# Streaming encoder layer, one core: the last query blocks' weight loads are asked for together, and the first head's second loads are placed behind them

## The chip, the cores and the metric

The kernel runs on one core of one Trainium2 chip. The metric is the device time of one execution in microseconds. Before the change the median of three runs is 2940.57 us (2935.65 to 2942.43).

## The reference, cut to what matters

One layer of a chunk-causal encoder, for 2048 new frames of one stream (16 tiles of 128 rows) and 16 frames of each of 8 running streams (one more tile, the sample tile). All arithmetic is float32.

```
h = rmsnorm(x, g_mix_pre)
proj = h @ w_in                       # 1024 -> q 512 | k 512 | v 512 | u_val 512 | u_gate 512
att = band_attention(q, k, v)         # 8 heads of 64, band of 9 chunks of 64, learned bias
u = u_val * sigmoid(u_gate)
c = depthwise_conv(u, width=31) + conv_b
c = silu(layernorm(c, cln_g, cln_b))
x = x + rmsnorm(concat(att, c) @ w_out, g_mix_post)
...                                   # cross-attention over 256 memory tokens, then a SwiGLU FFN
```

The outputs hold the new x, the keys and values of the band, and the convolution's last rows.

## The kernel before, in words

**Products.** A float32 product is made of three fast ones. Each operand is split into a high part (a rounding copy) and a low part (the rest), and high·high, high·low and low·high are added in PSUM. `mm3` issues the three, on lines 284, 285 and 286 of the profile. A block of weights, 128 columns by 1024 rows, goes through `wload`: a load on SP's queue into a buffer `wf` (L274), a rounding copy on ScalarE (ACT) into `wh` (L278), and the rest on POOL into `wl` (L279). There are three `wf` buffers and four each of `wh` and `wl`, used in turn. So a load waits until the block three earlier has been split, and a split waits until the products of the block four earlier are done.

**The projection** (`phase_proj`) takes the token tiles in three groups. The last group holds tiles 12 to 15 and the sample tile, in two parts of three and two tiles. For each group come the convolution's inputs (blocks 12 to 19 of `w_in`), the values, and then keys and queries. In the last group these are eight blocks, four of keys (called K0 to K3 here) and four of queries (Q0 to Q3), each of two heads. For each block and part `qk` multiplies (24 products of 384 columns, then 24 of 256), evicts the result from PSUM with ACT (L713 for keys, L707 for queries) and VectorE (L714, L708), and stores it in DRAM (L733); keys are also turned for the output (L721 to L726).

**The convolution** of the last group runs beside this, one step at a time: VectorE's taps are L524, POOL's and ACT's L534 and L533. Its end, `conv_norm`, is handed out in stages behind the products of Q1 and Q2. For each of the five tiles it transposes (L539, TensorE), takes statistics (L541 and L543 on VectorE, L299 and L302 on POOL), normalizes (L547), transposes back (L551), scales and applies tanh (L554, L557 on ACT) and multiplies (L558 on VectorE). POOL then stores the tile (L559). The last three of its five results lie at kilobytes 6 to 12 of the buffer `sbF`, which the second and third `wf` buffers also use.

**Attention's beginning.** For each head, `head_load` brings q, k, the low part of k and v back from DRAM (L809, L810). For the first head this is done in two parts: tiles 0 to 11 at the start of the last group, tiles 12 to 15 right after Q0. Scores are L894, the softmax is L822 on VectorE and L824 on ACT, its transposes are L911, their evictions L912 and L913, the products with the values L924. A sample stream's softmax uses the same lines with 272 columns, and bias rows that eight small loads (L937) bring. Those rows lie over the end of the second z tile of the convolution and the first columns of its tanh tile, so they can come only when the last L558 has run.

**What sets the order.** The program is written with a framework that places every instruction on its engine's queue, by the order of the code, by priorities and by its own model of time. Each engine then runs its queue strictly in that order. A load on SP that waits holds up all loads behind it. `issue_after(x)` asks that what is written inside it stand behind x.

Of the kernel before, what the change touches and what calls it, by code (L numbers as in the profile page):

```python
# [20 lines left out]
NPT = 16  # L21
# [116 lines left out]
class Build:  # L138
# [309 lines left out]
    def phase_proj(self):  # L448
        nc, A = self.nc, self.A
# [49 lines left out]
        def pump(q, n):  # L499
            while n > 0 and q:  # L500
                try:
                    with self.tc.high_priority(offset=-LOWP):
                        next(q[0])
                    n -= 1
                except StopIteration:
                    q.pop(0)
# [69 lines left out]
        def stage():  # L576
            if stages:
                with self.tc.issue_after(self.last_product.ins):
                    for i, n in stages.pop(0):
                        for _ in range(n):  # L580
                            next(staged[i], None)

        def stages_of(tiles, cts, tag, x):
            staged[:] = [conv_norm(t, cts, i * P, tag, x) for i, t in enumerate(tiles)]
            n = len(tiles)
            first = [tuple((i, 1) for i in range(x, min(n, x + 2))) for x in range(0, n, 2)] + [()]
            rest = [()] + [tuple((i, 2) for i in range(x, min(n, x + 2))) for x in range(0, n, 2)]
            stages.extend(r + f for r, f in zip(rest, first))
# [5 lines left out]
        for gi, subs in enumerate(GROUPS):  # L594
# [4 lines left out]
            t0 = tiles[0]  # L599
            hs = nxt  # L600
            if last:
                first = self.head_tiles(0)
# [131 lines left out]
                                                   sp[:, :, :npc].bitcast(F32))  # L734

            if last:
                for which, j in [(1, j) for j in range(4)] + [(0, j) for j in range(4)]:
                    blk = self.wload(A["w_in"][which * 4 + j])
                    for x in range(2):
                        qk(which, j, blk, x)  # L740
                        if (which, j, x) == (0, 1, 0):
                            while vq or pq:
                                pump(vq or pq, 1)
                            stages_of(tiles, cts, "nt", "x")
                        stage()
                    if (which, j) == (0, 0):
                        self.head_load(0, first, t0, NPT)
                        self.head0 = first
                break

            for j in range(3):
                for which in (1, 0):
                    blk = self.wload(A["w_in"][which * 4 + j])
# [1029 lines left out]
```

## Time and profile before

| | |
|---|---|
| three runs, median | 2940.57 us (2935.65, 2940.57, 2942.43) |
| the profiled execution | 2934.83 us |
| its span | 2933.1 us |
| TensorE's mean granted clock in it | 0.994 |
| the last group's end and attention's first head | about 560 to 670 us of the span |

In the rows of a timeline stand the start, the duration, the engine, the line and the operation, what is written and read, the shapes and how many follow each other; in brackets the idle time of that engine just before, and what ended it. PE is TensorE, DVE is VectorE, ACT is ScalarE, POOL is GpSimd, and SPq is SP's queue of DMA issues. In a row of stretches (start and end) stand the length, the busy time and the number of instructions of each engine, TensorE's granted clock, the share of the DMA engines and GB/s. In a row of waits stand who waited, for whom, how long in all, how often, and the longest.

### The profile page before, as it was taken

What the parts mean: (1) busy time and instruction counts of PE and PEld (TensorE: products, weight loads), DVE (VectorE), ACT (ScalarE), POOL (GpSimd) and SP (SyncE); (2) the same over time, 40 slices, a digit from 0 to 9 for tenths busy, and PEclk for the clock granted to TensorE, in tenths of its full rate; (3) what the DMA queues carried; (4) which work ended last, traced back from release to release, by engine and by line L of the source; (5) the groups of instructions that cost most, each with busy time, mean ns of one, the idle gap of its engine ahead of it and who ended that gap; (6) DMA issues with size and microseconds to landing.
All of it is one profiled execution on the core that took longest, in us unless ns stands there. A gap on an engine that the chain in (4) does not pass through costs nothing. (4 is left out here: it accounts for less than half of the span.)

```text
span 2933.1 us, 45413 instructions
## 1 busy us (share of the span) xinstructions
PE 2868.2 (98%) x16740; PEld 2623.9 (89%) x16740; DVE 2058.8 (70%) x3063; ACT 1311.1 (45%) x2661; POOL 1321.0 (45%) x1213
## 2 busy tenths in 40 slices
PE   8999999979999999999999999999999999999998
PEld 8999999979988777888889999999999999888787
DVE  6697796959985335345559877787778998556665
ACT  4535455749974234232334333433344444433433
POOL 0268595820023222233336665466556776324413
PEclk9999999989999999999999999999999999999999
DMA  8735255558855665133354433544444446756764
GB/s 305 252 112 173 97 167 180 158 158 199 212 161 183 208 244 173 51 130 106 138 167 154 177 129 110 198 159 148 143 153 149 142 141 222 232 174 219 247 200 150
DMA packets 198154, 500.04 MB, mean 170 GB/s; under 512 B 18981, under 2 KB 87085, under 8 KB 189603
## 3 DMA queue, kind: packets, MB, share of 16 engines
q1 hardware_dynamic: 187211, 459.78, 48.4%
q0 software_dynamic: 10720, 37.36, 3.3%
q8 instruction: 131, 2.15, 0.3%
q14 instruction: 92, 0.75, 0.1%
HBM read 365.97 MB, written 141.81 MB: 173 GB/s over the span
## 5 line engine op out<-in xcount | busy, mean ns | idle before, releaser
L284 PE MATMUL psb<-sbr 128*128 128x384 f32 (+3 forms) x2808 | 942.1, 337 | 14.2 <-ACT sbr L278 11.0
L285 PE MATMUL psb<-sbr 128*128 128x384 f32 (+3 forms) x2356 | 806.5, 342 | 2.4 <-DVE sbr L321 2.4
L286 PE MATMUL psb<-sbr 128*128 128x512 f32 (+3 forms) x1848 | 631.1, 344 | 2.6 <-DVE sbr L1685 2.5
L284 PEld LDWEIGHTS psb<-sbr 128*128 128x128 f32 x2808 | 530.9, 189 | 44.2 <-ACT sbr L278 11.4
L286 PE MATMUL psb<-sbr,sbx 128*128 128x384 f32 (+2 forms) x1484 | 477.2, 323 | 1.1 <-POOL sbx L279 1.0
L285 PEld LDWEIGHTS psb<-sbr 128*128 128x128 f32 x2356 | 445.6, 189 | 28.6 <-DVE sbr L321 2.7
L286 PEld LDWEIGHTS psb<-sbr 128*128 128x128 f32 x1848 | 347.6, 188 | 31.4 <-DVE sbr L1685 4.6
L1485 ACT CAST sbr<-sbf 128x512 fp32r<-128x512 f32 x258 | 159.3, 621 | 283.6 <-PE psb L285 249.1
L286 PEld LDWEIGHTS psb<-sbr,sbx 128*128 128x128 f32 x1484 | 281.5, 190 | 1.8 <-POOL sbx L279 1.7
L524 DVE SCALAR_TENSOR_TENSOR psb<-sbf,psb 128x768 f32<-128x768 f32 (+1 forms) x290 | 264.6, 912 | 6.6
L1486 DVE TENSOR_TENSOR sbr<-sbf,sbr 128x512 fp32r<-128x512 f32 x258 | 241.8, 940 | 28.0 <-ACT sbr L1485 26.3
L292 PE MATMUL psb<-sbr 128*128 128x512 f32 x1004 | 246.2, 394 | 2.8 <-ACT sbr L1053 1.6
L1685 DVE TENSOR_TENSOR sbr<-sbf,sbr 128x384 fp32r<-128x384 f32 (+1 forms) x231 | 161.1, 720 | 95.3 <-ACT sbr L1684 93.9
L292 PEld LDWEIGHTS psb<-sbr 128*128 128x128 f32 x1004 | 185.2, 188 | 44.5 <-issue 2.5
L279 POOL TENSOR_TENSOR sbx<-sbf,sbr 128x1024 fp32r<-128x1024 f32 x60 | 153.0, 2552 | 72.6 <-ACT sbr L278 72.2
L1684 ACT CAST sbr<-sbf 128x384 fp32r<-128x384 f32 (+1 forms) x231 | 111.0, 497 | 166.8 <-PE psb L285 141.8
L1617 POOL TENSOR_TENSOR sbf<-sbf 128x512 f32<-128x512 f32 x77 | 107.7, 1403 | 167.2 <-DMA sbf<-in_w_down_dram 165.0
L534 POOL TENSOR_TENSOR flexb<-flexb,flexb 128x128 f32<-128x128 f32 (+1 forms) x180 | 167.8, 933 | 18.6 <-ACT flexb L533 9.3
L284 PE MATMUL psb<-sbr,sbx 128*128 128x384 f32 (+1 forms) x524 | 171.1, 329 | 0.6 <-ACT sbr L1447 0.5
L1485 ACT CAST sbx<-sbf 128x512 fp32r<-128x512 f32 x153 | 94.8, 621 | 164.3 <-PE psb L285 152.7
L292 PE MATMUL psb<-sbr,sbx 128*128 128x512 f32 x654 | 161.5, 398 | 5.3 <-DVE sbr L1251 2.2
L292 PEld LDWEIGHTS psb<-sbr,sbx 128*128 128x128 f32 x654 | 123.3, 191 | 34.9 <-DVE sbr L1251 2.9
(333 smaller groups left out, 5907.7 us busy)
## 6 DMA issues: line engine op xcount, KB each, us to landing
af<-flexb SPq DMA_DIRECT2D x33, 1344.0 KB, 5.2
sbf<-in_w_down_dram SPq DMA_DIRECT2D x154, 256.0 KB, 3.6
sbf<-af SPq DMA_DIRECT2D x90, 384.0 KB, 4.2
sbf<-in_w_gate_dram SPq DMA_DIRECT2D x66, 512.0 KB, 4.8
sbf<-in_w_up_dram SPq DMA_DIRECT2D x66, 512.0 KB, 3.3
sbf<-in_w_in_dram SPq DMA_DIRECT2D x48, 512.0 KB, 3.9
sbf<-x SPq DMA_DIRECT2D x47, 512.0 KB, 3.9
sbr<-ks SPq DMA_DIRECT2D x28, 512.0 KB, 8.8
```

The lines of the kernel that those rows point to most:

```text
L279: self.lo_engine.tensor_tensor(lo[:, :], wf[:, :], hi[:, :].bitcast(F32), ALU.subtract)
L284: nc.tensor.matmul(ps, lh, rh, start=start, stop=False, **kw)
L285: nc.tensor.matmul(ps, lh, rl, start=False, stop=False, **kw)
L286: self.last_product = nc.tensor.matmul(ps, ll, rh, start=False, stop=stop, **kw)
L292: self.last_half = nc.tensor.matmul(y[o], l, r[:, o * 512:(o + 1) * 512], start=start and x == 0, stop=stop and x == 2)
L524: nc.vector.scalar_tensor_tensor(acc if w < CW - 1 else o, src(w), cwt[:, j, w:w + 1], acc, ALU.mult, ALU.add)
L534: nc.gpsimd.tensor_tensor(o, o, v, ALU.add)
L1485: nc.scalar.copy(hs[j][:, :], src[j])
L1486: nc.vector.tensor_tensor(ls[j][:, :], src[j], hs[j][:, :].bitcast(F32), ALU.subtract)
L1617: nc.gpsimd.tensor_tensor(acc[:, :], acc[:, :], q[:, :], ALU.add if s > 0 else ALU.subtract)
L1684: nc.scalar.copy(ch[:, m], a[:, x, m])
L1685: nc.vector.tensor_tensor(cl[:, m], a[:, x, m], ch[:, m].bitcast(F32), ALU.subtract)
```

## The change

When Q0 has been projected, the weights of Q1, Q2 and Q3 are asked for together, and the loop takes them from `ready` instead of loading each at its turn. The second part of the first head's loads is written inside `issue_after` of the last of these three loads.

```diff
             if last:
+                ready = {}
                 for which, j in [(1, j) for j in range(4)] + [(0, j) for j in range(4)]:
-                    blk = self.wload(A["w_in"][which * 4 + j])
+                    blk = ready.pop(j, None) or self.wload(A["w_in"][which * 4 + j])
                     for x in range(2):
                         qk(which, j, blk, x)
...
                     if (which, j) == (0, 0):
-                        self.head_load(0, first, t0, NPT)
+                        ready = {i: self.wload(A["w_in"][i]) for i in (1, 2, 3)}
+                        with self.tc.issue_after(self.last_load.ins):
+                            self.head_load(0, first, t0, NPT)
                         self.head0 = first
```

Three lines are added, so all lines below shift by three: L809 is L812 in the changed kernel, L822 is L825, L894 is L897, L913 is L916, L937 is L940.

On SP's queue the order of the loads was, around K0's store and, further on, around the bias loads:

```order
L274 DMA sbf<-in_w_in_dram 128x1024 x2
L733 DMA ks_14_86<-sbf 128x2x384
L695 DMA out_dram<-flexb_153 8x16x512
L733 DMA ks_14_86<-sbf 128x2x128
L809 DMA sbr<-ks_14_86 64x512 x4
L733 DMA ks_15_87<-sbf 128x2x384
```

```order
L834 DMA flexb_157<-in_cache_att_v_dram 128x2x512
L937 DMA flexb_153<-toep_595 16x272 x6
L274 DMA sbf<-in_w_in_dram 128x1024
L937 DMA flexb_153<-toep_595 16x272 x2
L1038 DMA flexb_153<-cs_36_108 128x512
```

The single L274 of the second piece is Q3's load; the two of the first are Q1's and Q2's. In the changed kernel the same two places read:

```order
L274 DMA sbf<-in_w_in_dram 128x1024 x2
L733 DMA ks_14_86<-sbf 128x2x384
L695 DMA out_dram<-flexb_153 8x16x512
L733 DMA ks_14_86<-sbf 128x2x128
L274 DMA sbf<-in_w_in_dram 128x1024
L812 DMA sbr<-ks_14_86 64x512 x3
L733 DMA ks_15_87<-sbf 128x2x384
L812 DMA sbr<-ks_14_86 64x512
L813 DMA sbr<-vs_18_90 128x512
```

```order
L841 DMA sbf<-in_cache_att_kt_dram 128x4x256
L836 DMA sbf<-vsampd_149 16x512
L837 DMA flexb_157<-in_cache_att_v_dram 128x2x512
L940 DMA flexb_153<-toep_595 16x272 x8
L1041 DMA flexb_153<-cs_36_108 128x512
```

Q3's load has gone from among the bias loads to a place ahead of the first head's second loads, and those, the value rows among them, now stand behind it.

On TensorE, this is the end of Q2 before and what followed it, and then the rows just ahead of the first product of Q3 (128x384):

```order
L286 MATMUL psb<-sbr,sbx 128x256
L894 MATMUL psb<-sbr 128x256 x2
L894 MATMUL psb<-sbr 128x512 x2
L551 MATMUL psb<-ident_73,flexb_153 128x128 x4
L539 MATMUL psb<-ident_73,flexb_157 128x128 x4
L894 MATMUL psb<-sbr 128x256 x2
```

```order
L894 MATMUL psb<-sbr 128x256 x2
L551 MATMUL psb<-ident_73,flexb_153 128x128 x4
L539 MATMUL psb<-ident_73,flexb_157 128x128 x4
L551 MATMUL psb<-ident_73,flexb_153 128x128 x4
L911 MATMUL psb<-ident_73,flexb_153 128x128 x2
L551 MATMUL psb<-ident_73,flexb_153 128x128 x4
L284 MATMUL psb<-sbr 128x384
```

In the changed kernel Q3's 48 products follow Q2's directly. Inside Q3's second part stand 16 transposes of the convolution, and after it the scores begin with tile 0:

```order
L284 MATMUL psb<-sbr 128x256
L551 MATMUL psb<-ident_73,flexb_153 128x128 x4
L539 MATMUL psb<-ident_73,flexb_157 128x128
L551 MATMUL psb<-ident_73,flexb_153 128x128 x4
L539 MATMUL psb<-ident_73,flexb_157 128x128 x7
L285 MATMUL psb<-sbr 128x256
```

```order
L286 MATMUL psb<-sbr,sbx 128x256
L897 MATMUL psb<-sbr 128x128 x2
L897 MATMUL psb<-sbr 128x256 x4
L551 MATMUL psb<-ident_73,flexb_153 128x128 x4
L539 MATMUL psb<-ident_73,flexb_157 128x128 x4
L897 MATMUL psb<-sbr 128x384 x2
```

So the scores and three of the five L551 groups, which stood ahead of Q3, now stand behind it.

On VectorE of the changed kernel, the last result of the convolution (L558) and the softmax of sample stream 0 (the 272 columns that use the bias rows) stand like this among the softmax tiles (L825, 640 columns) and the evictions (L916):

```order
L825 ISA flexb_153,flexb_157<-psb,flexb_153 128x640
L825 ISA flexb_157 128x1
L558 SCALAR_TENSOR_TENSOR sbf<-flexb_153,sbf 128x512
L916 TENSOR_TENSOR sbx<-psb,sbx 128x128
L916 TENSOR_TENSOR sbr<-psb,sbr 128x512
L916 TENSOR_TENSOR sbx<-psb,sbx 128x512
L825 ISA flexb_157<-psb,flexb_153 128x640
L825 ISA flexb_157 128x1
L916 TENSOR_TENSOR sbr<-psb,sbr 128x512
L825 ISA flexb_153,flexb_157<-psb,flexb_153 128x272
```

Before, all five L558 stood ahead of Q3's evictions, and the 272-wide softmax came after the sixth softmax tile; now nine tiles stand ahead of the last L558, and ten ahead of that softmax.

## Prediction

> **What bounds the kernel now.** First the page: TensorE is busy 98% of the span, so only a stage in which it stands idle can give much.
>
> ```profile
> span 2933.1 us, 45413 instructions
> PE 2868.2 (98%) x16740; PEld 2623.9 (89%) x16740; DVE 2058.8 (70%) x3063; ACT 1311.1 (45%) x2661; POOL 1321.0 (45%) x1213
> ```
>
> All times below are us from the span's start, of this one profiled execution: 2934.83 us on the device, 2933.1 of them span. The three timed runs have a median of 2940.57 (2935.65 to 2942.43); the profiled execution lies 5.7 below it.
>
> The change touches the end of the last group's projection, so I next read the busy time by stretches of 10 us there.
>
> ```profile
> core 0: us, PE busy (x) PEld busy (x) DVE busy (x) ACT busy (x) POOL busy (x), PEclk, DMA share, GB/s
> ...
> 610.00:620.00 10.00, 9.27 (x69) 8.66 (x68) 5.42 (x15) 3.05 (x10) 1.75 (x5) 1.00 0.48 158
> 620.00:630.00 10.00, 4.21 (x24) 2.87 (x22) 7.37 (x14) 9.61 (x26) 4.84 (x12) 0.81 0.59 202
> 630.00:640.00 10.00, 0.53 (x2) 0.54 (x3) 0.69 (x1) 1.82 (x3) 1.36 (x3) 0.50 0.62 212
> 640.00:650.00 10.00, 9.00 (x43) 8.71 (x42) 0.97 (x2) 0.49 (x1) 1.85 (x1) 0.67 0.17 43
> 650.00:660.00 10.00, 9.39 (x67) 7.80 (x65) 8.43 (x28) 7.48 (x21) 1.23 (x2) 1.00 1.02 236
> 660.00:670.00 10.00, 10.00 (x93) 9.19 (x92) 9.45 (x24) 9.66 (x26) 0.00 (x0) 1.00 0.45 92
> ```
>
> TensorE does nearly nothing from 620 to 640, its granted clock falls to 0.50 and is still 0.67 on average in the stretch after. The timeline of TensorE shows what stands around that hole.
>
> ```profile
> 608.51 0.34 PE L284 MATMUL psb<-sbr 128*128 128x384 f32 x1
> ...
> 616.08 0.40 PE L894 MATMUL psb<-sbr 128*128 128x256 f32 x2
> ...
> 627.38 1.06 PE L551 MATMUL psb<-ident,flexb 128*128 128x128 f32 x4
> 639.47 0.69 PE L284 MATMUL psb<-sbr 128*128 128x384 f32 x1 [11.03 <-ACT sbr L278]
> ...
> 650.52 0.28 PE L286 MATMUL psb<-sbr,sbx 128*128 128x256 f32 x1
> ```
>
> Block Q2 (third query block) starts at 608.51. At 616.08 TensorE, done with it, starts on scores of attention's first head (L894) mixed with the convolution's transposes (L551), waits 11.03 us for the weights of Q3, and does Q3 from 639.47 to about 650.64. Whose fault that is, the other engines' timelines and SP's waits say:
>
> ```profile
> 638.37 1.04 ACT L278 CAST sbr<-sbf 128x1024 fp32r<-128x1024 f32 x1 [7.56 <-DMA sbf<-in_w_in_dram]
> ```
> ```profile
> 631.56 2.68 SPq L937 DMA_DIRECT2D flexb<-toep  x6
> 634.61 0.36 SPq L274 DMA_DIRECT2D sbf<-in_w_in_dram  x1
> ```
> ```profile
> SPq L937 <- DMA cs<-flexb: 3.8, 1, 3.8
> ...
> SPq L937 <- DVE sbf L558: 0.4, 1, 0.4
> ...
> SPq L274 <- DMA cs<-sbf: 0.3, 1, 0.3
> ```
>
> Q3's load is issued only at 634.61. It stands behind six bias loads (L937), and it waits itself for a convolution result (cs) to be stored, because the convolution's z tiles lie on the weight buffers. So the hole is a late load and nothing else.
>
> **The change, part by part.** Of the three loads asked for together, Q1's and Q2's already stood in front; in SP's order only Q3's moves, from behind the bias loads to right behind K0's store. What it then waits for is a free `wf` buffer, that is Q0's low part on POOL:
>
> ```profile
> 571.90 2.39 POOL L279 TENSOR_TENSOR sbx<-sbf,sbr 128x1024 fp32r<-128x1024 f32 x1 [0.22 <-ACT sbr L278]
> ```
> ```profile
> 576.21 2.43 SPq L809 DMA_DIRECT2D sbr<-ks  x4
> ```
>
> The buffer is free at 574.29. The next entry of SP, the head's loads, left only at 576.21, so the new load fits into a wait that is there anyway. The pin on the head's loads therefore costs 0 by these rows; if POOL were later than 576.21, every microsecond would go to the loads behind it, which the attention first needs at 624, some 45 us later. [...]
>
> Q3's conversion must also wait for K3's products, whose `wh` and `wl` buffers it takes. They end just ahead of K3's last eviction:
>
> ```profile
> 593.34 0.27 ACT L713 CAST sbf<-psb 128x128 fp32r<-128x128 f32 x1
> ```
> ```profile
> 596.21 1.00 POOL L534 TENSOR_TENSOR flexb<-flexb,flexb 128x128 f32<-128x128 f32 x2 [0.23 <-ACT flexb L533]
> ...
> 610.08 0.24 POOL L842 COPY sbf<-flexb 128x64 f32<-128x64 f32 x1 [12.87 <-DVE flexb L524]
> ```
>
> So 1.04 us of ACT fall at about 593 and 2.4 us of POOL by 597, and Q3 is ready 19 us before it is needed at 616.08. The 2.4 us of POOL lie ahead of the last convolution taps, which end at 597.2; POOL then idles 12.87 us, and that covers them. Without the cover they would cost 2.4.
>
> Then TensorE goes from Q2 straight into Q3. Q2 took 608.51 to 616.08, 7.57 with five transposes (L539); Q3 is about 7.0 at full clock instead of 11.17, and with the 16 convolution transposes that now stand inside it ends at about 624.8. **What is late next** is no load: it is VectorE and ACT, which in the hole did the convolution's norms at leisure and now must do them together with the first softmax tiles. So I count VectorE's work.
>
> ```profile
> 620.15 0.70 DVE L541 BATCH_NORM_STATS2 flexb<-psb 128x6 f32<-128x512 f32 x1
> ...
> 621.59 0.78 DVE L547 TENSOR_SCALAR flexb<-psb,flexb 128x512 f32<-128x512 f32 x1
> ...
> 623.40 0.68 DVE L558 SCALAR_TENSOR_TENSOR flexb<-flexb 128x512 f32<-128x512 f32 x1
> ...
> 630.84 0.69 DVE L558 SCALAR_TENSOR_TENSOR sbf<-flexb,sbf 128x512 f32<-128x512 f32 x1 [1.36 <-ACT flexb L557]
> ...
> 652.51 0.83 DVE L849 COPY flexb<-flexb 64x64 f32<-64x64 f32 x4
> ...
> 654.31 0.44 DVE L822 CUSTOM_DVE_ANT_0 flexb<-psb,flexb 128x272 f32<-128x272 f32 x1
> ...
> 659.38 0.81 DVE L822 CUSTOM_DVE_ANT_0 flexb<-psb,flexb 128x640 f32<-128x640 f32 x1
> 660.12 0.08 DVE L822 DVE_READ_ACCUMULATOR2_ANT flexb<- 128x1 f32 x1
> 660.12 0.68 DVE L913 TENSOR_TENSOR sbr<-psb,sbr 128x512 fp32r<-128x512 f32 x1
> ```
>
> Q3's first half (three fifths of the 7.0) ends at 620.3; its eviction, two more batch statistics and a cast bring VectorE to about 624.1 (an estimate from these durations). By its new order it has then to do, up to the bias-dependent softmax of sample 0 (the 272-wide one): L547 three times 0.78, 2.3; L558 five times 0.69, 3.45; one L541 0.70 with its small follower 0.2; an eviction 0.3; six copies of L849 1.25; softmax of ten tiles, six full ones at 0.89 and four narrow ones by width, 5.3 + 1.9; L913 seven times, four of 512 at 0.68 and 768 columns more by width, 3.7; sample 0's softmax 0.53. Sum 19.6, so 643.7 without a wait. But the bias loads still wait for the last L558 (in before L558 ended at 631.53, the first bias load left at 631.56). It stands 3.6 ahead of the end of that list: 640.1. Eight bias loads at 0.45 take 3.6 (six took 2.68), and the last lands 2.4 later:
>
> ```profile
> DMA to landing us min/median/max: 2.1/2.4/3.5
> ```
>
> That is 646.1, plus 0.53: VectorE stands at **646.6** where sample 0, ten tiles and seven L913 are done. In before the tenth tile ends at 660.20 with five L913 done; with two more at 0.68 the same state is at 661.5. The difference is 14.9; I take 0.9 off for small waits between engines, **14 us**.
>
> Bounds. Above: TensorE's own work.
>
> ```profile
> 617.94 0.63 PE L551 MATMUL psb<-ident,flexb 128*128 128x128 f32 x4
> 618.40 0.60 PE L539 MATMUL psb<-ident,flexb 128*128 128x128 f32 x4
> ```
>
> Four transposes take 0.46, start to start. Of 616.08 to 650.64 (34.6 us) TensorE needs 7.0 for Q3, 3.7 for 32 transposes and about 2 for five pairs of early scores (0.40 for the pair at 616.08): 12.7, so the gain is at most 22. Below: VectorE may pack worse than without a gap. It was busy 8.43 of 10 in the nearest stretch, 650 to 660, and 7.37 in 620 to 630. At 0.74 the last L558 comes at 645.8 instead of 640.1, and 8 to 9 us are left. I take 14, since 9.45 of 10 in 660 to 670 shows that these very softmax steps pack densely.
>
> The clock comes back with this by itself: the row 630 to 640 shows 0.50 after the long wait. [...]
>
> **The rivals.**
> 1. *TensorE bounds the stretch*: VectorE's arrears are taken up by attention's slack (it idles half a microsecond in ten at 660 to 670) and the bias comes in time. Gain 18 to 22, 2918.5 to 2922.5 on the median's scale. Against it: the arrears come at the start, where TensorE has only two score buffers.
> 2. *Poor packing*, with ACT as late as VectorE. Gain 6 to 11: 2929.5 to 2934.5.
>
> ```profile
> 623.40 1.53 ACT L554 ACTIVATE sbf<-psb,sbf 128x128 f32<-128x128 f32 x4
> 624.77 0.68 ACT L557 ACTIVATE flexb<-flexb 128x512 f32<-128x512 f32 x1
> ...
> 657.08 0.85 ACT L824 ACTIVATE flexb<-flexb 128x640 f32<-128x640 f32 x1
> ```
>
> Ahead of the last L558 ACT has five norms at 2.2 and seven exponentials at up to 0.85: 17 us from 621, so it reaches 638, two microseconds ahead of VectorE's 640. Either can be the one that is late; against it, both lists are full of work and not of waits.
> 3. *The change does not do what it says*, or the gain is hidden: Q3's load could be early and its conversion late. For it speaks that the conversion needs K3's buffers; against it 19 us of slack. Within 5.9: 2934.7 to 2946.4.
> 4. *Slower*: the bias loads. All eight, and everything behind them in SP, stand behind the last L558, which now sits among ten softmax tiles instead of ahead of them. Each microsecond it is later than 640 costs one. The gain is used up at 654, and the kernel is slower by 5.9 us from 660 on: 2946.5 or more. For it: SP did wait there, 3.8 and 0.4. Against: ACT's 17 us ahead of it would have to become 32.
>
> **How the numbers follow.** 2934.83 − 14 = 2920.8 for an execution like the profiled one; on the scale of the median 2940.57 − 14 = 2926.6, I say 2926.5. Chances: forecast (gain 11 to 18) 0.62, rival 1 0.10, rival 2 0.13, rival 3 0.10, rival 4 0.05. The first three are faster by over 0.2% (5.9 us, about what a measurement of this kernel can tell from no change): 0.85, the same 0.10, slower 0.05. The range takes in both bounds and the spread of the runs: from 22 under the mean of the four known times, 2938.4, with a little for their spread, 2915, to 2936, just inside rival 3.
>
> **What would show it.** No wait of TensorE for L278 near 616 and a Q3 of 7 to 9 us that follows Q2; the load L274 at 574 to 577; Q3's conversion near 594; the scores of tile 0 (L897 there) near 625; the last L558 near 640 and the bias loads behind it; granted clock 1.00 throughout 610 to 660; the tenth softmax tile 14 to 16 us earlier than 660.2. I am wrong if the last L558 comes after 646, if TensorE's clock falls again between 625 and 647, or if the time saved there is lost in the rest of attention, whose order the change also shifts.

## The result, and the profile after

| kernel | median us | range | runs |
|---|---|---|---|
| before | 2936.34 | 2935.65 to 2942.43 | 6 |
| changed | 2927.88 | 2924.27 to 2932.13 | 6 |

The ratio is 0.9966, with a 95% interval of 0.9953 to 0.9979: 10.0 us faster, between 6.2 and 13.8, by the ratio, 8.5 by the two medians. The forecast was 2926.5, with a gain of 14 and a band of 11 to 18 for it: the time came within 1.4 us, the gain below the band. The profiled execution took 2932.13 us, 2930.4 of them span; it is the slowest of its six, while the profiled execution of before (2934.83) lies below all six that were timed.

Busy time by stretches of 10 us of the changed kernel, the columns as in the prediction (PE, PEld, DVE, ACT, POOL, then the granted clock):

```profile
610.00:620.00 10.00, 10.00 (x69) 10.00 (x69) 4.01 (x9) 1.60 (x5) 1.51 (x4) 1.00 0.59 196
620.00:630.00 10.00, 9.31 (x69) 7.88 (x67) 7.87 (x22) 8.42 (x25) 3.46 (x8) 1.00 1.03 234
630.00:640.00 10.00, 7.64 (x48) 5.16 (x47) 9.19 (x25) 10.00 (x26) 2.20 (x7) 1.00 1.04 345
640.00:650.00 10.00, 6.03 (x33) 4.88 (x33) 5.27 (x13) 5.12 (x12) 1.38 (x2) 0.85 0.42 145
650.00:660.00 10.00, 10.00 (x79) 9.05 (x78) 7.63 (x19) 7.75 (x18) 0.00 (x0) 0.81 0.08 14
660.00:670.00 10.00, 10.00 (x79) 8.99 (x78) 9.17 (x24) 9.39 (x25) 0.53 (x3) 1.00 1.02 225
```

The hole of 620 to 640 is filled. A smaller one has opened at 640 to 650, where TensorE, VectorE and ScalarE are all half idle, and the clock falls there and in the stretch after (0.85 and 0.81). First the timelines of the changed kernel that answer to the load: SP's load of Q3, ScalarE's and GpSimd's halves of its conversion, and TensorE's first product of Q3 and first scores.

```profile
574.09 0.34 SPq L274 DMA_DIRECT2D sbf<-in_w_in_dram  x1
```
```profile
592.83 1.03 ACT L278 CAST sbr<-sbf 128x1024 fp32r<-128x1024 f32 x1
```
```profile
593.94 2.41 POOL L279 TENSOR_TENSOR sbx<-sbf,sbr 128x1024 fp32r<-128x1024 f32 x1 [0.38 <-ACT sbr L278]
```
```profile
615.73 0.34 PE L284 MATMUL psb<-sbr 128*128 128x384 f32 x1
...
624.51 0.86 PE L897 MATMUL psb<-sbr 128*128 128x128 f32 x6
```

Load, conversion, Q3 and scores stand where the prediction put them (574 to 577, about 594, right behind Q2, near 625). Then what VectorE, SP and TensorE do at the new hole (in brackets the idle time ahead, and who ended it):

```profile
638.87 0.69 DVE L558 SCALAR_TENSOR_TENSOR sbf<-flexb,sbf 128x512 f32<-128x512 f32 x1
...
642.25 0.82 DVE L825 CUSTOM_DVE_ANT_0 flexb<-psb,flexb 128x640 f32<-128x640 f32 x1 [0.42 <-PE psb L914]
...
645.85 0.44 DVE L825 CUSTOM_DVE_ANT_0 flexb<-psb,flexb 128x272 f32<-128x272 f32 x1 [1.96 <-DMA flexb<-toep]
```
```profile
639.59 4.80 SPq L940 DMA_DIRECT2D flexb<-toep  x8
```
```profile
646.35 0.62 PE L897 MATMUL psb<-sbr 128*128 128x384 f32 x2 [1.75 <-DVE flexb L825]
648.28 1.44 PE L897 MATMUL psb<-sbr 128*128 128x384 f32 x4 [1.31 <-DVE flexb L825]
```

The last L558 ends at 639.56, SP sends the eight bias loads behind it, and VectorE, which takes its work in order, waits 1.96 us for them ahead of sample 0's softmax (272 columns). SP itself was held up twice between these loads:

```profile
SPq L940 <- DMA sbf<-in_cache_att_kt_dram: 0.7, 1, 0.7
SPq L940 <- DMA flexb<-in_cache_att_v_dram: 0.7, 1, 0.7
```

In the trace SP's loads take eight semaphores in turn, and the sixth and the eighth bias load wait until two loads of the sample's cache (L841 and L837, issued at 627.00 and 632.30), which had the same semaphores, have landed. So the eight took 4.80 from the first to the last, not the 3.6 of the prediction. TensorE has no free score buffer meanwhile and waits 1.75, then 1.31. The second row of TensorE says one thing more: four products of 384 columns took 1.44, where they took 0.85 at 639.01. The granted clock is halved (0.50 from 646.97 to 653.79).

**How much of the lead is kept.** Attention's order on VectorE has 136 softmax steps in both kernels, so the start of the 41st, far behind the place where the projection hands over to attention (the seam), can be compared. By then before, the changed kernel and e3 below have all issued the same 132 score products and 96 products with the values on TensorE, so this is a lead in work done and not in order. What differs by chance at the start of the program is taken off by a row ahead of the change (L692 on TensorE). TensorE, then VectorE, of before:

```profile
563.15 0.38 PE L692 MATMUL psb<-ident,sbf 128*128 128x128 f32 x2
```
```profile
705.94 0.82 DVE L822 CUSTOM_DVE_ANT_0 flexb<-psb,flexb 128x640 f32<-128x640 f32 x1
```

The same two rows of the changed kernel:

```profile
562.73 0.38 PE L692 MATMUL psb<-ident,sbf 128*128 128x128 f32 x2
```
```profile
696.09 0.82 DVE L825 CUSTOM_DVE_ANT_0 flexb<-psb,flexb 128x640 f32<-128x640 f32 x1
```

705.94 − 696.09 = 9.85, less 563.15 − 562.73 = 0.42: the changed kernel leads by **9.4 us** at the 41st softmax. That is the measure used below. At sample 0's softmax VectorE was done at 646.29 where the prediction said 646.6 and gave 661.5 for before, a lead of some 15. The 661.5 holds 1.4 us for two evictions (L913) that before does later; by the rows alone, sample 0's softmax and ten tiles are done at 660.20 and at 646.29, a lead of 13.5 with the 0.42 taken off. So some 4 us by this count, a good 5 by the prediction's, are given back between 646 and the 41st step. That is what the experiments had to explain.

### The profile page after: what moved, and what is told of

Read it like the earlier page. It is cut to its first block, busy times and chain, and to the rows that moved or that the text cites. A ratio compares the mean times of both kernels' runs of the same rounds, so it can differ in the third digit from the quotient of the medians.

```text
span 2930.4 us, 45410 instructions
## 1 busy us (share of the span) xinstructions
PE 2873.8 (98%) x16740; PEld 2626.0 (90%) x16740; DVE 2062.7 (70%) x3063; ACT 1311.0 (45%) x2661; POOL 1317.3 (45%) x1213
## 5 line engine op out<-in xcount | busy, mean ns | idle before, releaser
L284 PE MATMUL psb<-sbr 128*128 128x384 f32 (+3 forms) x2808 | 941.6, 337 | 2.9 <-ACT sbr L320 1.1
L284 PEld LDWEIGHTS psb<-sbr 128*128 128x128 f32 x2808 | 530.4, 189 | 32.6 <-ACT sbr L1687 2.1
L286 PEld LDWEIGHTS psb<-sbr,sbx 128*128 128x128 f32 x1484 | 280.5, 189 | 0.1
L284 PE MATMUL psb<-sbr,sbx 128*128 128x384 f32 (+1 forms) x524 | 170.9, 329 | 2.7 <-DVE sbf L1542 2.2
L1489 DVE TENSOR_TENSOR sbx<-sbf,sbx 128x512 fp32r<-128x512 f32 x153 | 145.2, 951 | 12.8 <-ACT sbx L1488 12.1
```

What stands on the lines that cost most here:

```text
L284: nc.tensor.matmul(ps, lh, rh, start=start, stop=False, **kw)
L286: self.last_product = nc.tensor.matmul(ps, ll, rh, start=False, stop=stop, **kw)
L1489: nc.vector.tensor_tensor(ls[j][:, :], src[j], hs[j][:, :].bitcast(F32), ALU.subtract)
```

## The experiments

Theory A: the forecast is right up to 646; what is given back behind it comes from VectorE's wait for the bias rows, which starves TensorE and halves its clock. Rival B: VectorE and ScalarE bound attention anyway, and the 15 was never a real lead. Theory C: the change costs time at later seams of the program. Two smaller questions: does the pin matter, and do the loads of Q1 and Q2?

Each run has its lead at the 41st softmax against before's profile (the subtraction above), its median and its ratio to the runs of before on the same chip.

| run | L692 | 41st softmax | lead | median us | ratio, 95% |
|---|---|---|---|---|---|
| changed kernel | 562.73 | 696.09 | 9.4 | 2927.88 | 0.9966 (0.9953 to 0.9979) |
| e1, the same again | 563.87 | 696.49 | 10.2 | 2930.14 | 0.9971 (0.9961 to 0.9981) |
| e12, the same again | 563.38 | 696.83 | 9.3 | 2927.46 | 0.9963 (0.9951 to 0.9975) |
| e2, no pin | 564.59 | 696.72 | 10.7 | 2929.76 | 0.9970 (0.9959 to 0.9982) |
| e5, Q3 stays | 562.21 | 704.85 | 0.2 | 2937.08 | 1.0000 (0.9991 to 1.0008) |
| e4, before with bias early | 564.54 | 705.67 | 1.7 | 2936.52 | 0.9995 (0.9986 to 1.0004) |
| e3, bias early | 562.95 | 691.10 | 14.6 | 2927.44 | 0.9964 (0.9951 to 0.9977) |
| e11, e3 again | 563.54 | 691.67 | 14.7 | 2926.76 | 0.9963 (0.9950 to 0.9975) |
| e6, bias twice | 563.33 | 704.08 | 2.0 | 2936.77 | 0.9993 (0.9984 to 1.0001) |
| e7, sample later | 564.73 | 695.40 | 12.1 | 2930.33 | 0.9969 (0.9959 to 0.9980) |
| e8, gate on GpSimd | 566.49 | 697.86 | 11.4 | 2927.16 | 0.9963 (0.9951 to 0.9975) |
| e9, no gate | 563.39 | 689.12 | 17.1 | 2927.59 | 0.9957 (0.9940 to 0.9975) |
| e10, one scale | 562.69 | 691.96 | 13.5 | 2928.94 | 0.9969 (0.9956 to 0.9982) |

The runs of before have medians of 2936.34, 2938.38, 2937.87 and 2936.96 in the four series. The lead repeats to within a microsecond; single times of one kernel spread over some 8 us, of before over 12.

### e1 and e12: the changed kernel again

No edit.

> The changed kernel once more, unaltered, for a second profile. Theory A (the gain is made by 646 us as forecast and a third of it is given back between 646 and 655, because VectorE waits for the sample bias rows and TensorE's clock halves): the sample's softmax over 272 columns starts near 645.9 again behind a wait of about 2 us for the bias loads, a half-clock stretch of 3.4 to 6.8 us follows near 647, and from softmax tile 40 to the end of attention the profile stands 9 to 11 us ahead of before's. Theory C (the gain is lost at later seams of the program, near 1585, 2470 and 2745 us, where the first profile of the change lost 3.5, 1.3 and 1.8 us, by the change itself): those losses come again. Under A they are chance (where the clock's windows fall on a wait) and at least one of the three does not come again. Time 2925 to 2930, ratio 0.996 to 0.9975.

> The change once more, unaltered, as the other side of that comparison: softmax tile 40 at 9.3 to 10.7 us ahead of before's profile (program start taken off), a wait of 1 to 2 us of VectorE for the bias loads, time 2927 to 2930.5.

Leads of 10.2 and 9.3. The 272-column softmax waits again for the bias, 1.33 and 1.87 us, and half clock follows at 649.7 and 648.0 (granted clock 0.84 in e1's stretch of 650 to 660, 0.76 in e12's). In e1 there is also half clock ahead of the wait, from 639.5 to 642.9 (0.97 in 630 to 640, 0.84 in 640 to 650). e2 below has the same order on VectorE there: these four executions, with waits of 1.15 (e2), 1.33, 1.87 and 1.96 us, have leads of 10.7, 10.2, 9.3 and 9.4, so by and large the longer wait goes with the smaller lead.

Against theory C there is a later seam at 1580, seen in stretches of 4 us (columns as above). First the changed kernel's first profile, then e1, which is the same program:

```profile
1582.00:1586.00 4.00, 1.85 (x8) 1.57 (x9) 4.00 (x8) 0.00 (x0) 1.65 (x3) 0.95 0.65 211
1586.00:1590.00 4.00, 4.00 (x16) 4.00 (x16) 3.19 (x7) 0.82 (x2) 0.00 (x0) 0.62 0.95 379
```
```profile
1582.00:1586.00 4.00, 3.35 (x19) 3.36 (x20) 4.00 (x9) 0.62 (x1) 0.36 (x1) 1.00 0.96 327
1586.00:1590.00 4.00, 4.00 (x25) 4.00 (x24) 4.00 (x8) 2.05 (x4) 1.86 (x2) 1.00 0.35 134
```

At equal instructions of TensorE, against before's profile, the first execution loses 3.9 us between 1585 and 1608 and e1 0.05. At 2470 both lose (2.3 and 2.6), e12 does not (0.06). So one program keeps or loses some microseconds at these seams from execution to execution. The medians, which average over this, say the same: the changed kernel gains 8.5, 8.2 and 9.5 us in the three series that have it, and its lead on TensorE near 968, ahead of these seams, is 9.3, 8.4 and 8.2. Theory C falls as a cost of the change. In the first profile 2.3 of its lead are left near 2900, which is why the spans of the two single profiles differ by only 2.7 us (2933.1 and 2930.4) while the medians differ by 8.5.

### e2: the pin taken away

```diff
-                        with self.tc.issue_after(self.last_load.ins):
+                        with ExitStack():
                             self.head_load(0, first, t0, NPT)
```

> The change without its second half: the second part of the first head's loads is no longer issued behind the last weight load. SP's order differs from the change by three loads of that head, two ahead of the Q3 load by one or two rows. My working (the pin costs and brings nothing, the early load does all): the Q3 load still issues at 574 to 578, its conversion still near 594, time within 1.5 us of the change. Rival (the pin is what makes room for the load): the Q3 load is late by more than 20 us, or the time goes back by 4 us or more toward before.

SP of e2:

```profile
578.34 0.53 SPq L274 DMA_DIRECT2D sbf<-in_w_in_dram  x1
```

The load goes out at 578.34 and has 16 us to its conversion (L278 at 594.69); lead 10.7, median 0.4 us from e1's. The pin neither costs nor brings anything that shows here, as was expected.

### e5: only Q3's load put back

```diff
-                        ready = {i: self.wload(A["w_in"][i]) for i in (1, 2, 3)}
+                        ready = {i: self.wload(A["w_in"][i]) for i in (1, 2)}
```

> The change without its third load: the weights of Q1 and Q2 are asked for together and the head's loads are pinned behind them, but Q3's weights are asked for where before asked for them. My working (only Q3's load carries the gain): the Q3 load goes again behind six bias loads near 634, TensorE waits about 11 us for it, clock 0.50 in 630 to 640; time within 2 us of before. Rival (the early loads of Q1 and Q2 or the pin bring part of the gain): at least 3 us below before, and softmax tile 40 stands over 2 us ahead of before's profile.

SP and TensorE of e5:

```profile
633.65 0.36 SPq L274 DMA_DIRECT2D sbf<-in_w_in_dram  x1
```
```profile
638.50 0.69 PE L284 MATMUL psb<-sbr 128*128 128x384 f32 x1 [11.68 <-ACT sbr L278]
```

The late load, the hole and the time of before are all back: ratio 1.0000, lead 0.2. The whole gain comes from Q3's load.

### e4: before, with the bias rows out of the way

The bias rows get a place of their own, and their loads go out behind the last key store. The edit is that of e3, below, made in the kernel before.

> The kernel before, with only the bias rows moved as in the third run: the Q3 load no longer stands behind six bias loads, but still waits for the store of the convolution result that lies on its buffer. That store lands about 634.6 by the 0.3 us that the load still waited behind the bias loads. If the buffer is what holds the load (my working): it issues at 634 to 634.6, TensorE waits until about 639, time within 1 us of before. If the bias loads hold it: it issues near 631.6, Q3 begins 3 us earlier, time 3 us below before.

SP of e4 (its program starts 1.4 us later than before's, so 635.55 is 634.2 on before's scale):

```profile
635.55 0.35 SPq L274 DMA_DIRECT2D sbf<-in_w_in_dram  x1
```

With six loads fewer ahead of it, Q3's load comes 0.45 earlier, not 3. What held it was the store of the convolution result on its buffer. The lead of 1.7 is over the microsecond that was expected of the time, but the time is the same within its interval. What brings the lead was not tried.

### e3 and e11: the change, with the bias rows early

```diff
-                    blk = ready.pop(j, None) or self.wload(A["w_in"][which * 4 + j])
+                    self.bias_after = self.last_load if which or not j else self.bias_after; blk = ready.pop(j, None) or self.wload(A["w_in"][which * 4 + j])
...
-                     .lay(fa, 0, ("qbd", 0.5, 2), ("osb", 0.5, 2)).lay(fa, 5, ("otmp", 2, 1), ("bs", 1.0625, 1)).lay(fa, 19, ("bt", 2.5, 2))
+                     .lay(fa, 0, ("qbd", 0.5, 2), ("osb", 0.5, 2)).lay(fa, 5, ("otmp", 2, 1)).lay(fa, 26.5, ("bs", 1.0625, 1)).lay(fa, 19, ("bt", 2.5, 2))
...
-            nc.sync.dma_start(bs[h * DEC_S:(h + 1) * DEC_S, :], toep[h][:DEC_S, PAST:2 * PAST + DEC_S])
+            with self.tc.issue_after(self.bias_after.ins): nc.sync.dma_start(bs[h * DEC_S:(h + 1) * DEC_S, :], toep[h][:DEC_S, PAST:2 * PAST + DEC_S])
...
-        pool = self.wp = Region().lay(self.fa, 27.5, ("eye", 0.03125, 1), ("rc", 0.03125, 2)).lay(
+        pool = self.wp = Region().lay(self.fa, 27.5625, ("eye", 0.03125, 1), ("rc", 0.03125, 2)).lay(
```

> The change, with the sample bias rows on a place of their own (they lay on the convolution's z and tanh tiles) and their eight loads issued behind the last key store, near 595 us, in a wait of SP. Theory A: the 272-column softmax loses its wait for the bias loads and comes at 643.5 to 644.5, no half clock near 647, and tile 40 stands 13 to 15.5 us ahead of before's profile where the change stands 9.85; time 3 to 5.5 us below the change, 2922 to 2925 on the same chip. Rival B (attention after 646 is bound by VectorE and ScalarE, whatever the sample waits for; the lead of 15 us at the sample's softmax was a difference of order and no real lead): tile 40 stands 9 to 11 ahead as in the change, and the time is within 1.5 us of it.

> The third run once more, unaltered, beside the change on the same chip, for a tighter interval. Theory A: softmax tile 40 at 14 to 15 us ahead of before's profile (program start taken off), time 3 to 5 us below the change. The seams after 850 us give or take 2 to 4 us by chance in each execution, so single times may cross.

VectorE of e3 at sample 0's softmax, and its stretch there:

```profile
640.51 0.43 DVE L825 CUSTOM_DVE_ANT_0 flexb<-psb,flexb 128x272 f32<-128x272 f32 x1
```
```profile
640.00:650.00 10.00, 9.33 (x75) 7.75 (x75) 7.61 (x18) 7.93 (x21) 1.53 (x2) 0.87 0.41 147
```

The wait for the bias is gone, the softmax comes 5.3 us sooner and TensorE is busy 9.33 of 10 instead of 6.03. The lead is 14.6 and 14.7, in the range that theory A gave, and rival B falls: a lead of that size can be kept. Two parts of the expectation missed. The softmax comes at 640.51, not at 643.5 to 644.5, because by e3's order it also stands one step sooner, as the tenth and not the eleventh. And the clock does halve here too, earlier (0.50 from 639.24 to 642.65), behind waits of TensorE for VectorE (0.93 and 0.27) and ScalarE (0.46) that have nothing to do with the bias. Since order and wait changed together, how the 5 us divide between them is open.

In time little of this arrives: medians of 2927.44 and 2926.76 beside the change's 2930.14 and 2927.46 on the same chips, 2.7 and 0.7 us better, not the 3 to 5.5 expected, and within the spread. Of the lead some 3 us are lost at the end of attention in both executions: at the 133rd softmax step it is 14.4 and 14.1, at TensorE's instructions near 968 in before it is 11.2 and 10.9; that of the changed kernel falls by 0.4 in two executions (9.7 to 9.3, 8.6 to 8.2) and by 1.9 in e1 (10.3 to 8.4). TensorE of e3, then of the changed kernel, at the first products of the stage behind attention:

```profile
853.46 4.85 PE L292 MATMUL psb<-sbr 128*128 128x512 f32 x13 [2.13 <-DVE flexb L825]
```
```profile
856.01 1.20 PE L292 MATMUL psb<-sbr 128*128 128x512 f32 x4 [1.60 <-ACT sbr L1056]
```

The moved softmax shifts attention's order, its last wait is longer, and the clock halves behind it in both executions (0.78 in 852 to 856 of e3, 0.80 of e11). The changed kernel's first profile has 1.00 there, but e1, the same program, halves from 857.9 to 861.3 (0.90 in 850 to 860, 0.93 in 860 to 870). So the longer wait and the clock are what the traces show there; that the new order causes them was not tried. e3 was not shown faster than the change.

### e6: twice the bias loads

```diff
-        for h in range(H):
+        for h in [x for x in range(H) for _ in range(2)]:
             nc.sync.dma_start(bs[h * DEC_S:(h + 1) * DEC_S, :], toep[h][:DEC_S, PAST:2 * PAST + DEC_S])
```

> The change with every bias load issued twice, which puts eight more loads of 0.6 us each in SP's queue ahead of the sample's softmax (4.8 us more). Theory A with the price that the prediction gave (each microsecond that the bias is later costs one): the 272-column softmax at 650 to 651 instead of 645.85, VectorE waiting 6 to 7 us for it, TensorE idle longer and half-clocked for at least two windows, softmax tile 40 at 4 to 6 us ahead of before's profile instead of 9.5 to 9.9, time 3.5 to 6 us above the change, 2932.5 to 2936. Rival B (attention takes the wait up): tile 40 at 9 to 10, time within 1.5 us of the change.

VectorE and TensorE of e6:

```profile
654.20 0.44 DVE L825 CUSTOM_DVE_ANT_0 flexb<-psb,flexb 128x272 f32<-128x272 f32 x1 [5.49 <-DMA flexb<-toep]
```
```profile
654.71 1.01 PE L897 MATMUL psb<-sbr 128*128 128x384 f32 x2 [7.34 <-DVE flexb L825]
```

The softmax comes later, the lead is smaller and the time longer than was expected, because the dose was larger. The fifteen loads ahead of the next other load took 10.77 us. Their issues were not slower (a median of 0.39 us for 0.41 in the changed kernel), but five times one of them waited for an earlier bias load to land:

```profile
SPq L940 <- DMA flexb<-toep: 4.4, 5, 3.1
```

So the softmax comes 7.7 us later than in the changed kernel (654.20 − 645.85, less 0.6 of program start), and the lead is 7.4 us smaller. The price is about one for one, next to nothing is taken up behind it, and nearly the whole gain of the change is gone: ratio 0.9993. Half clock runs during and behind the wait from 649.6 to 659.9 (0.51 in 650 to 660), and behind it for 6.83 us in the changed kernel.

### e7: sample 0 later

```diff
-            if i % NPT and (i % 2 == 0 or i > SLAST):
+            if i % NPT and (i % 2 == 0 or i > SLAST or i < NPT) and i > 7:
                 next(fill, None)
```

> The change with the steps of the first sample four tiles later (one at each of units 8 to 13 instead of at every second one from 2), the bias rows left where they are. By order the 272-column softmax then stands behind thirteen tiles instead of ten, 3 us more of VectorE's work, so that the bias has landed, or nearly, when it comes. Theory A (it is the wait for the bias in VectorE's queue, not the place of the rows): the wait of 1.3 to 2 us shrinks below 0.5, no half-clock stretch near 647, tile 40 at 12 to 15 ahead of before's profile, time 2 to 5 us below the change. Rival B: tile 40 at 9 to 10, no change of time.

VectorE of e7:

```profile
648.72 0.44 DVE L825 CUSTOM_DVE_ANT_0 flexb<-psb,flexb 128x272 f32<-128x272 f32 x1 [2.49 <-DMA flexb<-toep]
```

The expectation missed: the wait did not shrink, it grew to 2.49, since the bias landed later in this run (its program starts 2.0 us later than that of the changed kernel's profile, and the eight loads took 6.27 us instead of 4.80). The lead at the 41st softmax is larger all the same, 12.1. TensorE waits only 0.87 us behind it, and no half clock follows (1.00 in 650 to 660; the one half-clock stretch here lies at 639.4 to 642.8, with 0.97 in 630 to 640 and 0.86 in 640 to 650). So where the wait falls matters beside its length, as far as one run can show. But the new order loses the lead again, 8.4 at the 133rd step, and no time is gained. The lead of 12.1 is not rival B's 9 to 10, but since the wait did not shrink, the run does not test theory A as it was meant to.

### e8, e9, e10: who is late between 624 and 641

All three have the bias rows early, as in e3. The gate is the last product of the convolution (L558). e8 moves it to GpSimd, e9 leaves it out, and e10 replaces ScalarE's four scaled copies for each tile by one, without the gain and offset of each channel.

e8:

```diff
-            nc.vector.scalar_tensor_tensor(z[:, :, :], th[:, :, :], 1.0, z[:, :, :], ALU.add, ALU.mult)
+            (nc.gpsimd.tensor_tensor(th[:, :, :], th[:, :, :], z[:, :, :], ALU.mult), nc.gpsimd.tensor_tensor(z[:, :, :], th[:, :, :], z[:, :, :], ALU.add)) if x else nc.vector.scalar_tensor_tensor(z[:, :, :], th[:, :, :], 1.0, z[:, :, :], ALU.add, ALU.mult)
```

e9:

```diff
-            nc.vector.scalar_tensor_tensor(z[:, :, :], th[:, :, :], 1.0, z[:, :, :], ALU.add, ALU.mult)
+            None if x else nc.vector.scalar_tensor_tensor(z[:, :, :], th[:, :, :], 1.0, z[:, :, :], ALU.add, ALU.mult)
```

e10:

```diff
-            for j in range(4):
-                nc.scalar.activation(z[:, j, :], pz[:, j, :], AF.Identity, scale=half[:, 0, j:j + 1],
-                                     bias=half[:, 1, j:j + 1])
+            for j in range(0 if x else 4):
+                nc.scalar.activation(z[:, j, :], pz[:, j, :], AF.Identity, scale=half[:, 0, j:j + 1], bias=half[:, 1, j:j + 1])
+            None if not x else nc.scalar.activation(z[:, :, :], pz[:, 0:4, :], AF.Copy, scale=0.5)
```

> The third run (bias rows early) with the last group's gate of the convolution (L558, five times 0.69 us) taken from VectorE and done on GpSimd as a product and a sum. If VectorE is what is late between 624 and 641, as the prediction's sum has it: the scores and softmax tiles there come up to 3.4 us earlier, tile 40 at 16.5 to 18.5 ahead of before's profile instead of 14.8, time 1.5 to 3 us below the third run. If ScalarE is late (it is busy 10.00 of 10 in 630 to 640, VectorE 9.19): tile 40 within 1 us of the third run, no change of time. If the two are matched: in between.

> The third run with the last group's gate of the convolution (L558 on VectorE, five times 0.69 us) left out, so that the convolution output of that group lacks its factor; nothing takes its place on another engine. VectorE is what is late between 624 and 641 (the prediction's sum): softmax tile 9 and tile 40 come 2 to 3.5 us further ahead than in the third run (17.3 and 14.6, program start taken off). ScalarE is late: within 1 us of the third run.

> The third run with the four scaled copies for each convolution tile of the last group (L554, ScalarE, 1.5 to 1.9 us for a tile) replaced by one copy with factor 0.5 (about 0.67), so that the per-channel gain and offset are left out; ScalarE has some 4.5 to 6 us less to do between 615 and 637. ScalarE is what is late there (busy 10.00 of 10 from 630 to 640): softmax tile 9 and tile 40 come 3 to 5 us further ahead than in the third run, and TensorE is busier than 9 of 10 from 630 to 640. VectorE is late: within 1 us of the third run. Both matched: 1 to 2 us.

GpSimd of e8, its last gate instruction:

```profile
648.46 1.27 POOL L558 TENSOR_TENSOR sbf<-flexb,sbf 128x512 f32<-128x512 f32 x1
```

e8 came out as none of the cases expected, and tells nothing of VectorE. GpSimd takes two times 1.3 us a tile, its gates end at 649.7 instead of 639.6 (its program starts 3.8 us later), and sample 0's small copies (L845) stand in GpSimd's queue between them; the lead falls to 11.4. e9 and e10 put the question cleanly. Their stretches of 630 to 640, beside that of e3: e3, e9 and then e10:

```profile
630.00:640.00 10.00, 7.64 (x44) 5.22 (x45) 9.18 (x25) 10.00 (x27) 2.29 (x6) 0.96 1.03 334
```
```profile
630.00:640.00 10.00, 7.34 (x43) 5.88 (x43) 7.81 (x24) 10.00 (x28) 2.37 (x8) 0.87 1.02 346
```
```profile
630.00:640.00 10.00, 7.26 (x38) 5.56 (x38) 8.24 (x23) 7.32 (x18) 3.09 (x8) 0.83 1.02 312
```

Without VectorE's 3.45 us the lead grows by 2.4, to 17.1. With several microseconds less on ScalarE, which falls from 10.00 to 7.32 of 10, it does not grow: 13.5 at the 41st step, and at the tenth 17.3 as in e3, with some 3.4 us more at half clock (0.83 in 630 to 640 and in 640 to 650, for 0.96 and 0.87 in e3), worth at most 1.7 (an estimate: half of the 3.4). The engine that reads 10.00 of 10 is not the one that is late here; VectorE is. In time this does not show: medians of 2927.59 and 2928.94 beside 2926.76 of e11 on the same chip.

## Why the prediction was right, and what was mis-sized

**Right, with the number beside it.** Only Q3's load carries the gain (e5). The load fits into SP's wait (574.09), and the pin costs nothing (e2). The conversion is covered (592.83 and 593.94), and Q3 follows Q2 at 615.73 without a wait. From 624 to 641 VectorE is late, not a load (e9, e10); only behind that do the bias loads hold it, as the sum has it. The sum holds to a microsecond: last L558 at 639.56 for 640.1, sample 0's softmax done at 646.29 for 646.6. The last step of it holds by luck: the eight loads took 4.80 for 3.6, and the softmax started 1.5 us behind the last issue's end, where the sum has 2.4 for the landing. Rival 4's price, a microsecond for each that the bias is later, was right in size (e6, 7.4 us of lead for 7.7), though the case did not come. That Q3's buffer and not the bias loads ahead of it held the load in before is shown by e4.

**The term that was mis-sized** is the last line of the sum: "The difference is 14.9; I take 0.9 off for small waits between engines, 14 us". It took VectorE's lead at 646.6 for the kernel's lead. At that moment VectorE had waited 1.96 us for the bias, which the sum did count, but TensorE stood still behind it, which the sum did not. Its waits of 1.75 and 1.31 and then the half clock came on top. The lead kept is 9.3 to 10.2 in three executions; with the wait taken out, and the order changed a little, it is 14.6 and 14.7 (e3, e11). So the term should have been about 5 instead of 0.9.

**The signs that failed.** The first is "granted clock 1.00 throughout 610 to 660". Stretches of the changed kernel of 3.41 us each, laid on the two edges at which the granted clock changed here (646.97 and 653.79):

```profile
640.14:643.55 3.41, 2.51 (x17) 1.92 (x15) 2.10 (x5) 1.79 (x5) 0.25 (x1) 1.00 0.85 309
643.55:646.97 3.42, 1.67 (x10) 1.11 (x9) 1.46 (x5) 2.23 (x6) 0.00 (x0) 1.00 0.34 95
646.97:650.38 3.41, 2.10 (x9) 2.10 (x10) 1.95 (x5) 0.96 (x3) 0.98 (x1) 0.50 0.01 2
650.38:653.79 3.41, 3.41 (x16) 3.13 (x15) 2.17 (x5) 2.28 (x6) 0.00 (x0) 0.50 0.00 0
653.79:657.21 3.42, 3.42 (x45) 2.93 (x45) 2.30 (x6) 3.22 (x7) 0.00 (x0) 1.00 0.00 0
```

In the 3.42 us from 643.55 TensorE was busy 1.67, with one wait of 1.75, and the next 6.83 us ran at half clock: 2.10 + 3.41 us of products at half rate, up to 2.8 us lost by that (an estimate: half of their 5.51). The sum counts no loss of clock behind the wait for the bias; the runs showed one. Before's own profile has a case of that size: half clock begins at 2247.54, 1.3 us after the end of a wait of TensorE of 1.8 us (L284 for L1541). In e1 the clock fell at 639.5 already (0.97 in 630 to 640), inside the 625 to 647 that the prediction named as a sign of being wrong.

The second is small: the tenth softmax tile ends at 643.07, 17.1 us ahead of 660.20 and not 14 to 16, because in the new order it stands ahead of sample 0's softmax.

**Rivals.** Rival 1 (gain 18 to 22) is out: TensorE was busy 7.64 of 10 in 630 to 640, not full. Rival 4's case did not come, since L558 stayed at 640. Rival 3 is out by e5 and by the rows at 592.83 and 593.94. Rival 2 named the size that came, 6 to 11, but not by its mechanism: VectorE packed 9.19 of 10 in 630 to 640, and ScalarE was not late.

**The predicted time** was near for a second reason. It started from 2940.57, the median of the three runs shown; longer series of before give 2936.3 to 2938.4. A base 2 to 4 us too high and a gain some 5 us too large nearly cancelled. That "the time saved there is lost in the rest of attention", which I named as a way to be wrong, did happen, for a third of the lead, and right at its start: from the 41st to the 133rd step the lead of the changed kernel stays at 9.4 to 9.7.

**Open.** How the 5 us divide between TensorE's waits, the half clock and the order of the softmax steps was not separated: e3, e7 and e6 each change the order too. Ahead of the hole nothing is lost: the first instruction behind Q2 starts at 616.08 before, and at 615.73 + 0.42 = 616.15 in the changed kernel.

## What to carry to other kernels

When a hole in the bottleneck engine is closed, what stood in that hole unseen, here eight small loads that a buffer conflict pins behind the last tile of another stage, becomes the next wait. Look for what the following work needs that was only ready because the hole was there, and free it in the same change. And a lead that is worked out on one engine is the kernel's lead only if the others are not starved at that moment: count what the bottleneck engine loses behind the wait too, its refill and its clock.

## What the runs showed of the hardware that was not expected

The granted clock fell behind short waits of TensorE: one of 1.75 us ahead of 646.97 in the changed kernel, and waits of 0.46, 0.93 and 0.27 ahead of 639.24 in e3. In the profiles of before and of the changed kernel, leaving out the last 20 us of the program, half clock begins nine times: at 626.21, 1138.21 and 2247.54 in before, and at 646.97, 1128.25, 1148.73, 1585.63, 2240.99 and 2469.68 in the changed kernel. It lasts 3.41 us six times, 6.83 twice and 20.48 once. In the 3.41 us ahead of each, as long as the shortest of them, TensorE was busy 1.42, 0.73 and 1.61 us, and 1.67, 1.01, 1.48, 1.48, 1.61 and 1.43; in e3 it was 1.85. What sets the clock was not tried.

The same waits go with half clock in one execution and not in the next. In e1 and in the first profile of the change, which are one program, half clock begins behind the bias wait near 649.7 and at 646.97, some 85.8 and 84.2 us behind the row of L692. At the end of attention TensorE waits 0.59 and 1.60 us in the first profile (1.00 in 852 to 860) and 0.60 and 1.61 in e1, and only e1's clock halves (0.90 in 850 to 860).

What the small loads cost in SP's queue were issues and waits, and the waits made the difference. Eight bias loads took 4.80 us in the changed kernel, six took 2.68 in before and fifteen 10.77 in e6, but a single issue took 0.30 to 0.55 in all three. The rest is waiting for earlier loads to land (0.7 and 0.7 in the changed kernel, 4.4 in e6). In the changed kernel the two loads of the sample's cache landed some 15.6 and 11.8 us after their issue, after a stretch in which its DMA share reads 1.03 to 1.04. One issue in that stretch held SP for 3.20 us:

```profile
629.00 3.20 SPq L836 DMA_DIRECT2D sbf<-vsampd  x1
```
